# Gate projections by Strassen's seven products as well, sums of weights in one chain per set

## The chip, the core and the metric

The kernel runs on one core of a Trainium2 chip. The core has TensorE (PE: matrix products, its weight loads shown as PEld), VectorE (DVE), ScalarE (ACT), GpSimd (POOL) and SyncE (SP, which here only starts DMA transfers). They run side by side and wait for each other by semaphores; each takes its own instructions in order. The metric is the device time of one execution in microseconds (us), the median of several runs.

## The reference

A two-layer encoder on 512 tokens of width 1024, all in float32. Each layer:

```
x = x + 0.5 * swiglu(rms_norm(x, ffn1_norm), w_gate, w_up, w_down)     # d_ff = 2816
z = rms_norm(x, mix_norm) @ w_in;  four attention mixers;  x = x + y @ w_out
x = x + 0.5 * swiglu(rms_norm(x, ffn2_norm), w_gate, w_up, w_down)
x = x + sigmoid(rms_norm(x, ple_norm) @ w_gate) * (p @ w_proj)
swiglu(u) = (silu(u @ w_gate) * (u @ w_up)) @ w_down
```

and a last RMSNorm. The change touches the two matrices `w_gate` and `w_up` of the four FFNs (two a layer).

## The kernel before

Tokens lie along the free dimension (512 columns), features along the 128 partitions. A float32 product is made of three matmuls of rounded operands: weights and activations are each split into a high and a low part, and high x high, high x low and low x high are accumulated (`mm3`, `product`). A weight block is loaded raw by SP and then **cut** (`cut`, L223): ScalarE writes the rounded high part `wh` (L231), VectorE subtracts it to get the low part `wl` (L232). There are three buffers of `wh` and three of `wl`. `take` hands a cut block to TensorE and prepares the next ones, two ahead in the FFN.

An FFN has 22 blocks of 128 gate and up columns, done in two halves of 12 and 10 blocks (`CUT`), each half followed by its part of the down projection (8 output tiles, each over the blocks `hs[0:4]`, `hs[4:8]`, `hs[8:]`). Blocks 0 and 1 of the first half are computed directly; meanwhile `combos` makes sums of activations in tiles TC. From then on blocks go in pairs (10 pairs per FFN, 40 in all). In a pair:

- **up** of both blocks goes by Strassen's scheme in Winograd's form (`seven`): the weights of the two blocks are a 2 x 2 matrix of 512 x 128 pieces a11, a12, a21, a22, the tokens are halved into 256 columns, and 7 products of 256 columns (named X1, Z1, X2, Y, X3, Z2, X4; each is 12 matmuls, L407) take the place of 8. Three PSUM banks X, Y, Z collect them; X takes four products, read out between them. ScalarE and VectorE put the results together in `u` (L422 to L434).
- **gate** of both blocks is direct: 4 half blocks of 12 matmuls with 512 columns (L298 to L300), then `gate` per block: multiplication by the norm factor `rb` (L440), Tanh (L442), one scalar_tensor_tensor (L443).
- `ORDER` = "ssdssdssdsd" sets how TensorE goes through the 7 products (s) and the 4 direct halves (d). The first block is multiplied by up and split for the down projection after Z2 (L514), the second at the end (L516).

The products need sums of weight pieces. `sums` and `factors` make them by DMA: SP loads a piece into a buffer `y` (L249), and accumulating DMAs, which only the POOL queue issues, add others (L251, L266): S1 = a21 + a22, S2 = S1 + a11 in a buffer of its own, S3 = a11 + a21, S4 = S2 + a12 in S2's buffer. That is five accumulations per pair. The `y` tag has four buffers.

What sets the order: instructions of TensorE and SP stay as written (`manual_schedule`). Those of the other engines are ordered at build time by a list scheduler, which takes older instructions first among those that it counts as ready; `hold` keeps the written order only in the opening. SP therefore stops at a load whose buffer isn't free, and all later loads wait behind it.

Of the kernel before, what the change touches and what calls it, by code (L numbers as in the profile page):

```python
# [17 lines left out]
T = 512  # L18
KC = 8
FF = 22  # L20
HT = 256
CUT = (0, 12, 22)
S_STEPS = ("X1", "Z1", "X2", "Y", "X3", "Z2", "X4")
ORDER = "ssdssdssdsd"
EPS = 1e-6
BIG = 1e30
NT_MIX = 20
# [10 lines left out]
class Encoder:  # L38
# [47 lines left out]
        return self.tile("keep", [128, 2, T], F32R, 7)  # L86

    def ytile(self):
        return self.tile("y", [128, T], F32, 4)

    def dense(self):
        return self.ps.tile([128, T], F32, tag="ps", name=self.nm("ps"), bufs=3)

    def small(self):
        return self.ps.tile([128, T], F32, tag="s", name=self.nm("s"), bufs=4)

    def either(self):
        self.turn ^= 1
# [19 lines left out]
    def setup_mix(self):  # L118
        nc, a, c = self.nc, self.a, self.const
        self.sink = c.tile([128, self.depth, 4], F32, name="sink")  # L120
        nc.sync.dma_start(self.sink, a["sink"])
        self.nsink = c.tile([128, self.depth, 4], F32, name="nsink")
        nc.gpsimd.tensor_scalar(out=self.nsink, in0=self.sink, scalar1=-1.0, scalar2=None, op0=ALU.mult)
        self.na_mask = c.tile([128, 7, 16], F32, name="na_mask")
        nc.sync.dma_start(self.na_mask, a["na_mask"])
        self.swa_mask = c.tile([128, 384], F32, name="swa_mask")
        nc.sync.dma_start(self.swa_mask, a["swa_mask"])
        self.dil_mask = c.tile([128, 896], F32, name="dil_mask")
        nc.sync.dma_start(self.dil_mask, a["dil_mask"])
        self.klz = [c.tile([128, 2, T], F32R, name=f"klz{i}") for i in range(2)]  # L130
        self.nkl = 0
        for t in self.klz:
            nc.gpsimd.memset(t[64:128, 0].bitcast(F32), 0.0)
            nc.gpsimd.memset(t[0:64, 1].bitcast(F32), 0.0)

    def g(self, l, off, k):
        c = l * GAINS + off + k
# [17 lines left out]
    def plan(self):  # L155
        a = self.a
        full = ((0, 4, 128), (512, 4, 128))
        for l in range(self.depth):
            for w in range(2):
                gu = a["ffn_gu"][l, w]  # L160
                for half in range(2):
                    c0, c1 = CUT[half], CUT[half + 1]
                    for f in range(c0, c1, 2):
                        if f == 0:
                            for n, g in enumerate(self.direct(l == w == 0, gu)):
                                yield g
                                if n == 4:
                                    sums = self.sums(gu[2, 1], gu[3, 1])
                            continue
                        s = self.factors(gu[f, 1], gu[f + 1, 1], sums)  # L170
                        d = self.slices((gu[f, 0], full), (gu[f + 1, 0], full))
                        for n, c in enumerate(ORDER):
                            yield s if c == "s" else d
                            if n == 3 and f + 2 < FF:
                                sums = self.sums(gu[f + 2, 1], gu[f + 3, 1])
                    for m in range(KC):
                        dn = a["ffn_d"][l, w, m]
                        yield from self.each((dn[:, c0:c0 + 8], full), (dn[:, c0 + 8:c1], ((0, c1 - c0 - 8, 128),)))
                if w == 0:
                    for i in range(M_END):  # L180
# [32 lines left out]
    def opening_pieces(self, gu):  # L213
        nc, a = self.nc, self.a
        for i, (k, e, xs) in enumerate(((0, 0, (0,)), (0, 1, (1, 2, 3)), (4, 0, (4,)), (4, 1, (5, 6, 7)))):
            raw = self.raw()[:, 0:512]
            src = gu[0, e][:, k:k + 4]
            nc.sync.dma_start(raw, src.rearrange("p k m -> p (k m)"))
            for m in xs:
                nc.sync.dma_start(self.x[m], a["x"][:, m])  # L220
            yield self.cut(raw, 4, self.own("TC", [128, 2, T], F32R, 8))

    def cut(self, r, k, both=None):  # L223
        nc = self.nc
# [13 lines left out]
            for o, k, m in cuts:  # L238
                yield self.cut(raw[:, o:o + k * m], k)

    def sums(self, a, b):

        flat = lambda src, k: src[:, k:k + 4].rearrange("p k m -> p (k m)")
        a11, a12, a21, a22 = flat(a, 0), flat(a, 4), flat(b, 0), flat(b, 4)
        nc = self.nc

        def load(first, *more):
            t = self.ytile()
            nc.sync.dma_start(t, first)  # L249
            for src in more:  # L250
                nc.gpsimd.dma_start(t, src, accum_op=ALU.add)  # L251
            return t

        s1 = load(a21, a22)
        s2 = load(a21, a22, a11)
        return s1, s2, lambda: load(a11, a21), a12

    def factors(self, a, b, sums):
        s1, s2, third, a12 = sums
        raw, half = self.load(a), self.raw()  # L260
        yield self.cut(raw[:, 0:512], 4)
        s3 = third()
        yield self.cut(s1, 4)
        self.nc.sync.dma_start(half[:, 0:512], b[:, 4:8].rearrange("p k m -> p (k m)"))
        yield self.cut(s2, 4)
        self.nc.gpsimd.dma_start(s2, a12, accum_op=ALU.add)  # L266
        yield self.cut(raw[:, 512:1024], 4)
        yield self.cut(s3, 4)
        yield self.cut(s2, 4)
        yield self.cut(half[:, 0:512], 4)  # L270

    def side(self):
        return self.nc.gpsimd if self.mixing else self.nc.vector
# [65 lines left out]
    def rspread(self, rc, tag="rb", bufs=1):  # L339
        nc = self.nc  # L340
        bc = self.spread(rc)
        rb = self.own(tag, [128, T], F32, bufs) if tag == "P" else self.tile(tag, [128, T], F32, bufs)
        nc.scalar.activation(rb, bc, AF.Copy)  # L343
        return rb

# [28 lines left out]
    def combos(self, l, off, j):  # L374
# [9 lines left out]
        nc.vector.scalar_tensor_tensor(f[:, 3], f[:, 2], -1.0, q[:, 2], op0=ALU.mult, op1=ALU.subtract)  # L384
        out = []
        for i in (0, 2):
            t = self.own("TC", [128, 2, T], F32R, 8).rearrange("p e (h t) -> p e h t", h=2)
# [22 lines left out]
    def seven(self, xs, tn, u):  # L410

        nc = self.nc
        bank = {}
# [49 lines left out]
    def ffn(self, l, w, nxt):  # L463
# [4 lines left out]
        tn, held = [], []  # L468
        for half in range(2):
            nf = CUT[half + 1] - CUT[half]  # L470
            hs = [self.big() if f < 7 else self.keep() for f in range(nf)]
            for f in range(2 if half == 0 else 0):
                gp, up = self.dense(), self.small()
                if l == w == f == 0:
# [16 lines left out]
            if half == 0:  # L491
                tn = [self.combos(l, off, j) for j in range(4)]
            for f in range(0 if half else 2, nf, 2):
                u = self.keep().bitcast(F32)
                s = self.seven(xs, tn, u)
                gps, grs, nd = [None] * 2, [None] * 2, 0
                for c in ORDER:
                    if c == "d":
                        e, part = divmod(nd, 2)
                        nd += 1  # L500
                        if part == 0:
                            gps[e] = self.dense()
                            self.mm3(gps[e], self.take(), xs[0:4], stop=False)
                            continue
                        self.mm3(gps[e], self.take(), xs[4:8], start=False)
                        grs[e] = self.gate(gps[e], rb)
                        continue
                    name = next(s)
# [4 lines left out]
                    if name == "Z2":  # L513
                        nc.vector.tensor_tensor(grs[0], grs[0], u[:, 0], op=ALU.mult)  # L514
                        self.split(hs[f], grs[0])
                nc.vector.tensor_tensor(grs[1], grs[1], u[:, 1], op=ALU.mult)  # L516
                self.split(hs[f + 1], grs[1])
            if self.sink is None:
                self.setup_mix()
            if half:  # L520
# [142 lines left out]
    def pv(self, h, b):  # L663
        nc, odd = self.nc, h["odd"]
        if b == 0:
            h["pv"] = self.ps.tile([128, T], F32, tag="pv", name=self.nm("pv"), bufs=1)
        pv = h["pv"]
        t0, t1 = self.span(h, b)
        c = slice(t0 * 128, t1 * 128)
# [224 lines left out]
    def mix(self, l, nxt):  # L894
# [244 lines left out]
def _prepare(i):  # L1139
# [7 lines left out]
    gu[:, :, 2:, 1] = gu[:, :, 2:, 1][:, :, :, :, [0, 2, 4, 6, 1, 3, 5, 7]]  # L1147
# [64 lines left out]
```

## Time and profile before

| | |
|---|---|
| median of 3 runs | 2111.67 us (2108.23 to 2111.96) |
| profiled execution | 2106.58 us |
| its span, first to last instruction | 2104.8 us |
| TensorE busy | 2058.1 us (98%), granted clock 0.995 |
| VectorE, ScalarE, POOL busy | 65%, 52%, 19% |
| DMA | 269.07 MB, 128 GB/s in the mean |

"Busy" counts the time in which an engine has at least one instruction running. Matmuls overlap in their pipeline, so the duration of one is longer than the time from its start to the next start. The four FFNs with their Strassen stretches lie at about 33 to 135 and 203 to 310, 660 to 768 and 830 to 938, 1075 to 1177 and 1243 to 1350, 1700 to 1805 and 1871 to 1977 us; behind each lies its part of the down projection.

### The profile page before, as it was taken

The page shows a single profiled execution, that of the slowest core. Times are in us where ns is not written, and L with a number is a line of the kernel's source. Part 1 is how long each engine was busy: PE and PEld are TensorE (multiplying, and loading weights), DVE is VectorE, ACT ScalarE, POOL GpSimd, SP SyncE. Part 2 cuts the span into 40 slices and gives each one's busy share as a digit, 9 for nine tenths or more (in the row PEclk, how much of TensorE's full clock was granted, in tenths as well). Part 3 has the DMA queues.
Part 4 walks back from the last instruction along what each step waited for, and adds up shares of the span by engine and source line. Part 5 has one row for each costly group of instructions (what it writes and reads, how often), then busy time and mean ns, then how long its engine had stood idle before and what let it go on. Part 6 is the DMA issues. An engine that isn't in the chain of part 4 may idle for free.

```text
span 2104.8 us, 29990 instructions
## 1 busy us (share of the span) xinstructions
PE 2058.1 (98%) x11012; PEld 1762.0 (84%) x11012; DVE 1364.0 (65%) x2269; ACT 1086.1 (52%) x2054; POOL 391.6 (19%) x390
## 2 busy tenths in 40 slices
PE   8999999999999999999999999999999899999997
PEld 7988988887877988988889889888878689889886
DVE  7654666778777654666866546667777766546664
ACT  6442444687864442444644334447787645334443
POOL 2200101043222200101121002011423312012011
PEclk9999999999999999999999999999999999999998
DMA  7764753322125754753467457433121367458332
GB/s 221 178 166 116 185 137 113 95 66 81 60 71 133 196 138 127 184 135 103 129 152 184 126 142 182 119 107 107 60 67 61 87 163 181 121 138 196 110 100 78
DMA packets 109605, 269.07 MB, mean 128 GB/s; under 512 B 12689, under 2 KB 16913, under 8 KB 109457
## 3 DMA queue, kind: packets, MB, share of 16 engines
q1 hardware_dynamic: 79232, 208.89, 31.4%
q0 software_dynamic: 30080, 58.21, 16.3%
q8 instruction: 86, 1.41, 0.3%
q14 instruction: 63, 0.51, 0.1%
q10 hardware_dynamic: 144, 0.05, 0.0%
HBM read 262.91 MB, written 2.10 MB: 126 GB/s over the span
## 4 chain that ended last, share of the span: by engine, by line
PE 43%; DVE 4%; ACT 1%; issue 1%; DMA 1%; POOL 0%; POOLq 0%; DVEq 0%; SPq 0%; ACTq 0%
PE s L407 8%; PE ps L299 7%; PE ps L298 7%; PE ps L300 7%; PE s L298 3%; PE s L299 3%; PE s L300 3%; PE ps L407 1%; PE pv L672 1%; PE s L656 1%; ACT tmp L542 0%; DVE PT L660 0%; PE s L614 0%; PE s L615 0%; DVE act L565 0%
## 5 line engine op out<-in xcount | busy, mean ns | idle before, releaser
L231 ACT ACTIVATE wh<-raw 128x512 fp32r<-128x512 f32 (+2 forms) x668 | 407.4, 612 | 569.1 <-PE ps L299 245.5
L232 DVE TENSOR_TENSOR wl<-raw,wh 128x512 fp32r<-128x512 f32 (+2 forms) x594 | 416.8, 703 | 258.3 <-ACT wh L231 251.1
L251 POOL DMA_DIRECT2D y<-in_ffn_gu x160 | 139.1, 878 | 909.0 <-DMA y<-in_ffn_gu 512.8
L298 PE MATMUL ps<-big,wh 128*128 128x512 f32 x632 | 252.4, 399 | 0.0
L299 PE MATMUL ps<-big,wh 128*128 128x512 f32 x632 | 247.9, 392 | 2.0 <-DVE big L152 2.0
L300 PE MATMUL ps<-big,wl 128*128 128x512 f32 x632 | 247.4, 391 | 1.6 <-DVE wl L232 1.6
L298 PE MATMUL ps<-act,wh 128*128 128x512 f32 x624 | 248.8, 399 | 0.0
L300 PE MATMUL ps<-act,wl 128*128 128x512 f32 x624 | 244.1, 391 | 1.4 <-DVE wl L232 1.4
L299 PE MATMUL ps<-act,wh 128*128 128x512 f32 x624 | 244.4, 392 | 0.6 <-DVE act L152 0.6
L407 PE MATMUL s<-TC,wh 128*128 128x256 f32 x1280 | 236.1, 282 | 0.7 <-ACT rb L343 0.7
L407 PEld LDWEIGHTS s<-TC,wh 128*128 128x128 f32 x1280 | 205.7, 189 | 10.3 <-ACT rb L343 0.9
L232 DVE TENSOR_TENSOR wl<-y,wh 128x512 fp32r<-128x512 f32 x160 | 110.8, 693 | 127.2 <-ACT wh L231 125.4
L407 PE MATMUL s<-TC,wl 128*128 128x256 f32 x640 | 181.4, 283 | 0.0
L231 ACT ACTIVATE wh<-y 128x512 fp32r<-128x512 f32 x160 | 101.2, 633 | 154.4 <-DMA y<-in_ffn_gu 60.7
L300 PEld LDWEIGHTS ps<-big,wl 128*128 128x128 f32 x632 | 118.6, 188 | 28.5 <-DVE wl L232 2.7
L300 PEld LDWEIGHTS ps<-act,wl 128*128 128x128 f32 x624 | 117.1, 188 | 27.3 <-DVE wl L232 1.8
L299 PEld LDWEIGHTS ps<-big,wh 128*128 128x128 f32 x632 | 119.2, 189 | 22.8 <-DVE big L152 3.1
L232 POOL TENSOR_TENSOR wl<-raw,wh 128x512 fp32r<-128x512 f32 (+1 forms) x74 | 95.8, 1295 | 216.2 <-ACT wh L231 210.0
L298 PEld LDWEIGHTS ps<-big,wh 128*128 128x128 f32 x632 | 119.2, 189 | 19.9
L299 PEld LDWEIGHTS ps<-act,wh 128*128 128x128 f32 x624 | 117.6, 188 | 20.8 <-DVE act L152 1.3
L298 PEld LDWEIGHTS ps<-act,wh 128*128 128x128 f32 x624 | 117.5, 188 | 19.6
L314 POOL TENSOR_TENSOR acc<-acc,tmp 128x512 f32<-128x512 f32 x48 | 66.9, 1394 | 344.7 <-ACT tmp L313 344.5
(230 smaller groups left out, 4343.9 us busy)
## 6 DMA issues: line engine op xcount, KB each, us to landing
raw<-in_ffn_gu SPq DMA_DIRECT2D x134, 512.0 KB, 5.1
y<-in_ffn_gu POOLq DMA_DIRECT2D x200, 256.0 KB, 4.9
raw<-in_ffn_d SPq DMA_DIRECT2D x64, 512.0 KB, 3.5
y<-in_ffn_gu SPq DMA_DIRECT2D x120, 256.0 KB, 3.9
raw<-in_w_in SPq DMA_DIRECT2D x40, 512.0 KB, 3.6
raw<-in_ffn_gu SPq DMA_DIRECT2D x44, 256.0 KB, 3.7
raw<-in_ffn_d SPq DMA_DIRECT2D x32, 256.0 KB, 2.7
raw<-in_w_out SPq DMA_DIRECT2D x16, 512.0 KB, 3.5
```

Of the source, the lines that this page charges most:

```text
L231: self.hold(nc.scalar.activation(hi, r, AF.Copy))
L232: self.hold(self.side().tensor_tensor(out=lo, in0=r, in1=hi.bitcast(F32), op=ALU.subtract))
L251: nc.gpsimd.dma_start(t, src, accum_op=ALU.add)
L298: nc.tensor.matmul(ps, lhsT=wh[:, k], rhs=x[:, 0], start=start and k == 0, stop=False)
L299: nc.tensor.matmul(ps, lhsT=wh[:, k], rhs=x[:, 1], start=False, stop=False)
L300: nc.tensor.matmul(ps, lhsT=wl[:, k], rhs=x[:, 0], start=False, stop=stop and k == last)
L314: self.hold(eng.tensor_tensor(out=acc, in0=acc, in1=sq, op=ALU.add))
L407: nc.tensor.matmul(ps, lhsT=v[:, k], rhs=x[:, e], start=start and k == i == 0, stop=k == 3 and i == 2, skip_group_check=True)
L656: nc.tensor.transpose(tp[:, t * 128:(t + 1) * 128], h["P"][t][:, o:o + 128], self.ident)
L672: nc.tensor.matmul(pv[:, c], lhsT=vb, rhs=h["pt"][b][:, i, c], start=b == 0 and i == 0, stop=b == 3 and i == 1, skip_group_check=True)
```

## The change

Gate goes through `seven` as well, as a second set with a buffer `g` beside `u`, and the products of the two sets take turns (up, gate, up, ...): 14 products per pair in place of 7 products and 4 direct halves. The order within a set becomes Z1, X1, Y, X2, X3, Z2, X4. The multiplication by `rb`, Tanh, the product with `u` and the split come after the fourteenth product, for both blocks together (1024 columns for the two multiplications). Gate's Y uses the bank `pv`, which only the mixer used.

The sums of a set share one buffer from a new tag S with seven buffers: S1 = a21 + a22, then a11 is added in place by DMA after S1 was cut, then a12 is added in place by VectorE after S2 was cut. S3 has its own buffer, and a22 is loaded alone. That is three accumulations per set, six per pair. The first two loads of the next pair's chains are issued after the eighth take of a pair. Buffers y, S, TC and klz now belong to stages (klz is cleared in each mixer stage), and the gate weights are laid out in DRAM as up's.

```diff
-S_STEPS = ("X1", "Z1", "X2", "Y", "X3", "Z2", "X4")
-ORDER = "ssdssdssdsd"
+S_STEPS = ("Z1", "X1", "Y", "X2", "X3", "Z2", "X4")
...
-                        s = self.factors(gu[f, 1], gu[f + 1, 1], sums)
-                        d = self.slices((gu[f, 0], full), (gu[f + 1, 0], full))
-                        for n, c in enumerate(ORDER):
-                            yield s if c == "s" else d
-                            if n == 3 and f + 2 < FF:
-                                sums = self.sums(gu[f + 2, 1], gu[f + 3, 1])
+                        fs = [self.factors(gu[f, i], gu[f + 1, i], chains[i]) for i in range(2)]
+                        for n in range(14):
+                            yield fs[1 - n % 2]
+                            if n == 7 and f + 2 < FF:
+                                chains = self.chains(gu, f + 2)
...
+    def block(self, *srcs):
+
+        t = self.own("S", [128, T], F32, 7)
+        for i, src in enumerate(srcs):
+            self.more(t, src, i > 0)
+        return t
+
+    def more(self, t, src, add=True):
+        src = src.rearrange("p k m -> p (k m)")
+        if add:
+            self.nc.gpsimd.dma_start(t, src, accum_op=ALU.add)
+        else:
+            self.nc.sync.dma_start(t, src)
+
+    def chains(self, gu, f):
+        c = [None, None]
+        for i in (1, 0):
+            b = gu[f + 1, i]
+            c[i] = self.block(b[:, 0:4], b[:, 4:8])
+        return c
+
+    def factors(self, a, b, s):
+        raw = self.load(a)
+        yield self.cut(s, 4)
+        self.more(s, a[:, 0:4])
         yield self.cut(raw[:, 0:512], 4)
+        s3 = self.block(a[:, 0:4], b[:, 0:4])
         yield self.cut(raw[:, 512:1024], 4)
+        a22 = self.block(b[:, 4:8])
+        yield self.cut(s, 4)
+        self.nc.vector.tensor_tensor(out=s, in0=s, in1=raw[:, 512:1024], op=ALU.add)
         yield self.cut(s3, 4)
+        yield self.cut(s, 4)
+        yield self.cut(a22, 4)
...
-                bank[b] = (self.dense() if b == "Y" else self.small())[:, :HT]
+                bank[b] = (self.small() if b == "X" else self.dense() if b == "Z" or first else self.extra())[:, :HT]
...
-            hs = [self.big() if f < 7 else self.keep() for f in range(nf)]
+            hs = [self.big() if f < 8 else self.keep() for f in range(nf)]
...
+                u, g = self.keep().bitcast(F32), (self.keep() if f % 4 else self.pair()).bitcast(F32)
+                su, sg = self.seven(xs, tn, u, True), self.seven(xs, tn, g, False)
+                for _ in S_STEPS:
+                    next(su)
                     if rc is not None:
                         rb, rc = self.rspread(rc), None
                         for j, hj in enumerate(held):
                             self.gated(*hj, rb, hs[j])
+                    next(sg)
+                nc.vector.tensor_tensor(g, g, rb.unsqueeze(1).to_broadcast([128, 2, T]), op=ALU.mult)
+                for e in range(2):
+                    th = self.tmp()
+                    nc.scalar.activation(th, g[:, e], AF.Tanh, scale=0.5)
+                    nc.vector.scalar_tensor_tensor(g[:, e], th, 1.0, g[:, e], op0=ALU.add, op1=ALU.mult)
+                nc.vector.tensor_tensor(g, g, u, op=ALU.mult)
+                for e in range(2):
+                    self.split(hs[f + e], g[:, e])
...
         self.stage("mx")
+        self.clear()
```

## Rows read from the trace of the kernel before

**Rows 1.** The page, part 1: busy us, share of the span, instructions.

```profile
PE 2058.1 (98%) x11012; PEld 1762.0 (84%) x11012; DVE 1364.0 (65%) x2269; ACT 1086.1 (52%) x2054; POOL 391.6 (19%) x390
```

**Rows 2.** Busy us by stretch (Strassen, down, Strassen); then PEclk, DMA share, GB/s.

```profile
60.00:121.00 61.00, 61.00 (x385) 55.28 (x384) 38.29 (x64) 29.04 (x54) 11.89 (x15) 1.00 0.76 187
145.00:195.00 50.00, 50.00 (x223) 41.40 (x221) 19.73 (x31) 12.02 (x19) 0.90 (x1) 1.00 0.37 108
1099.00:1161.00 62.00, 62.00 (x390) 56.10 (x389) 39.54 (x65) 30.67 (x56) 12.00 (x14) 1.00 0.76 184
```

**Rows 3.** Instructions in order of time, TensorE: start, duration in us, instruction, count.

```profile
82.37 0.40 PE L407 MATMUL s<-TC,wh 128*128 128x256 f32 x2
...
83.81 0.40 PE L407 MATMUL ps<-act,wh 128*128 128x256 f32 x2
...
85.24 0.40 PE L298 MATMUL ps<-act,wh 128*128 128x512 f32 x1
...
87.99 0.40 PE L407 MATMUL s<-TC,wh 128*128 128x256 f32 x2
```

**Rows 4.** The same view: VectorE at the pair's end, and one cut.

```profile
79.59 0.69 DVE L516 TENSOR_TENSOR tmp<-tmp,keep 128x512 f32<-128x512 f32 x1
...
83.93 0.63 ACT L231 ACTIVATE wh<-y 128x512 fp32r<-128x512 f32 x1 [0.90 <-PE s L407]
...
84.60 0.69 DVE L232 TENSOR_TENSOR wl<-y,wh 128x512 fp32r<-128x512 f32 x1 [0.84 <-ACT wh L231]
...
85.32 0.33 SPq L249 DMA_DIRECT2D y<-in_ffn_gu  x1
...
100.65 0.68 DVE L516 TENSOR_TENSOR tmp<-tmp,keep 128x512 f32<-128x512 f32 x1
```

**Rows 5.** Groups by line and shape: busy us, mean ns of one.

```profile
L232 DVE TENSOR_TENSOR wl<-y,wh 128x512 fp32r<-128x512 f32 x160 | 110.8, 693 | 127.2 <-ACT wh L231 125.4
...
L428 DVE TENSOR_TENSOR keep<-keep,ps 128x256 f32<-128x256 f32 x40 | 16.8, 421 | 6.2 <-PE ps L407 6.2
...
L865 DVE TENSOR_TENSOR raw<-na_mask,raw 128x896 f32<-128x896 f32 x8 | 8.7, 1090 | 1.6 <-DMA raw<-in_na_bias 1.6
...
L231 ACT ACTIVATE wh<-y 128x512 fp32r<-128x512 f32 x160 | 101.2, 633 | 154.4 <-DMA y<-in_ffn_gu 60.7 <-PE s L407 56.2 <-PE ps L300 13.4
...
L426 ACT ACTIVATE keep<-s 128x256 f32<-128x256 f32 x40 | 14.7, 367 | 0.0
```

**Rows 6.** In order of time, VectorE back to back.

```profile
109.36 0.69 DVE L232 TENSOR_TENSOR wl<-y,wh 128x512 fp32r<-128x512 f32 x1 [2.44 <-ACT wh L231]
109.96 0.69 DVE L440 TENSOR_TENSOR tmp<-ps,rb 128x512 f32<-128x512 f32 x1
...
111.16 0.42 DVE L430 TENSOR_TENSOR keep<-keep,s 128x256 f32<-128x256 f32 x1
111.49 0.69 DVE L443 SCALAR_TENSOR_TENSOR tmp<-tmp,tmp 128x512 f32<-128x512 f32 x1
```

**Rows 7.** The page, part 3: queue, packets, MB, share of 16 engines' span.

```profile
q1 hardware_dynamic: 79232, 208.89, 31.4%
q0 software_dynamic: 30080, 58.21, 16.3%
```

**Rows 8.** In order of time: SP's loads into y, POOL's accumulations waiting for them.

```profile
71.52 4.31 SPq L249 DMA_DIRECT2D y<-in_ffn_gu  x2
...
76.17 0.86 POOL L251 DMA_DIRECT2D y<-in_ffn_gu  x1 [5.90 <-DMA y<-in_ffn_gu]
...
91.66 5.23 SPq L249 DMA_DIRECT2D y<-in_ffn_gu  x2
...
95.80 0.86 POOL L251 DMA_DIRECT2D y<-in_ffn_gu  x1 [4.78 <-DMA y<-in_ffn_gu]
```

**Rows 9.** From issue to landing: L266 (x40) first, L251 (x160) second.

```profile
DMA to landing us min/median/max: 3.7/6.6/8.2
...
DMA to landing us min/median/max: 3.5/4.6/8.2
```

More of the change, by code (lines that the diff above doesn't have):

```diff
@@ L88, in ytile @@
     def ytile(self):
-        return self.tile("y", [128, T], F32, 4)
+        return self.own("y", [128, T], F32, 4)
     def dense(self):
@@ L95, in small, with extra, pair @@
         return self.ps.tile([128, T], F32, tag="s", name=self.nm("s"), bufs=4)
+    def extra(self):
+        return self.ps.tile([128, T], F32, tag="pv", name=self.nm("pv"), bufs=1)
+    def pair(self):
+        return self.own("TC", [128, 2, T], F32R, 9)
     def either(self):
@@ L129, in setup_mix, with clear @@
         nc.sync.dma_start(self.dil_mask, a["dil_mask"])
-        self.klz = [c.tile([128, 2, T], F32R, name=f"klz{i}") for i in range(2)]
+    def clear(self):
+        self.klz = [self.own("klz", [128, 2, T], F32R, 2) for _ in range(2)]
         self.nkl = 0
         for t in self.klz:
-            nc.gpsimd.memset(t[64:128, 0].bitcast(F32), 0.0)
-            nc.gpsimd.memset(t[0:64, 1].bitcast(F32), 0.0)
+            self.nc.gpsimd.memset(t[64:128, 0].bitcast(F32), 0.0)
+            self.nc.gpsimd.memset(t[0:64, 1].bitcast(F32), 0.0)
     def g(self, l, off, k):
@@ L166, in plan @@
                                 yield g
-                                if n == 4:
-                                    sums = self.sums(gu[2, 1], gu[3, 1])
+                                if n == (4 if l == w == 0 else 6):
+                                    chains = self.chains(gu, 2)
                             continue
-                        s = self.factors(gu[f, 1], gu[f + 1, 1], sums)
-                        d = self.slices((gu[f, 0], full), (gu[f + 1, 0], full))
-                        for n, c in enumerate(ORDER):
-                            yield s if c == "s" else d
-                            if n == 3 and f + 2 < FF:
-                                sums = self.sums(gu[f + 2, 1], gu[f + 3, 1])
+                        fs = [self.factors(gu[f, i], gu[f + 1, i], chains[i]) for i in range(2)]
[3 more added lines that the diff above has]
+                                chains = self.chains(gu, f + 2)
                     for m in range(KC):
@@ L220, in opening_pieces @@
                 nc.sync.dma_start(self.x[m], a["x"][:, m])
-            yield self.cut(raw, 4, self.own("TC", [128, 2, T], F32R, 8))
+            yield self.cut(raw, 4, self.pair())
     def cut(self, r, k, both=None):
@@ L239, in slices @@
                 yield self.cut(raw[:, o:o + k * m], k)
[L241 to L260, printed above, removed]
-        yield self.cut(raw[:, 0:512], 4)
[L262 to L266, printed above, removed]
+    def block(self, *srcs):
[19 more added lines that the diff above has]
+        self.more(s, a[:, 0:4])
+        yield self.cut(raw[:, 0:512], 4)
+        s3 = self.block(a[:, 0:4], b[:, 0:4])
         yield self.cut(raw[:, 512:1024], 4)
+        a22 = self.block(b[:, 4:8])
+        yield self.cut(s, 4)
+        self.nc.vector.tensor_tensor(out=s, in0=s, in1=raw[:, 512:1024], op=ALU.add)
         yield self.cut(s3, 4)
-        yield self.cut(s2, 4)
-        yield self.cut(half[:, 0:512], 4)
+        yield self.cut(s, 4)
+        yield self.cut(a22, 4)
     def side(self):
@@ L341, in rspread @@
         bc = self.spread(rc)
-        rb = self.own(tag, [128, T], F32, bufs) if tag == "P" else self.tile(tag, [128, T], F32, bufs)
+        rb = self.tile(tag, [128, T], F32, bufs) if tag == "rb" else self.own(tag, [128, T], F32, bufs)
         nc.scalar.activation(rb, bc, AF.Copy)
@@ L386, in combos @@
         for i in (0, 2):
-            t = self.own("TC", [128, 2, T], F32R, 8).rearrange("p e (h t) -> p e h t", h=2)
+            t = self.pair().rearrange("p e (h t) -> p e h t", h=2)
             nc.scalar.activation(t[:, :, 0], f[:, i:i + 2], AF.Copy)
@@ L408, in product, with seven @@
                                  stop=k == 3 and i == 2, skip_group_check=True)
-    def seven(self, xs, tn, u):
+    def seven(self, xs, tn, u, first):
         nc = self.nc
@@ L493, in ffn @@
             for f in range(0 if half else 2, nf, 2):
[L494 to L508, printed above, removed]
+                u, g = self.keep().bitcast(F32), (self.keep() if f % 4 else self.pair()).bitcast(F32)
+                su, sg = self.seven(xs, tn, u, True), self.seven(xs, tn, g, False)
+                for _ in S_STEPS:
+                    next(su)
                     if rc is not None:
@@ L512, in ffn @@
                             self.gated(*hj, rb, hs[j])
[L513 to L517, printed above, removed]
+                    next(sg)
[7 more added lines that the diff above has]
+                    self.split(hs[f + e], g[:, e])
             if self.sink is None:
@@ L665, in pv @@
         if b == 0:
-            h["pv"] = self.ps.tile([128, T], F32, tag="pv", name=self.nm("pv"), bufs=1)
+            h["pv"] = self.extra()
         pv = h["pv"]
@@ L1146, in _prepare @@
     gu = gu.reshape(L, 2, 2, KC, 128, FF, 128).transpose(0, 1, 5, 2, 4, 3, 6).copy()
-    gu[:, :, 2:, 1] = gu[:, :, 2:, 1][:, :, :, :, [0, 2, 4, 6, 1, 3, 5, 7]]
+    gu[:, :, 2:] = gu[:, :, 2:][:, :, :, :, :, [0, 2, 4, 6, 1, 3, 5, 7]]
     r["ffn_gu"] = gu
```

## The prediction

> **What bounds the kernel now.** I read the page's engine line first, then the busy time by stretch, then the order of time inside one pair of gate and up blocks, and last the DMA views. TensorE is busy 98% of the span [rows 1]. In the Strassen stretches it is busy in every one of the 61 or 62 us at a granted clock of 1.00, VectorE in 38 to 40 of them, ScalarE in 29 to 31, with the DMA engines at 76% [rows 2]. So in these stretches a weight or a buffer that comes late is not what ends a wait: the number of columns that TensorE streams sets the time. That is what the change cuts, and the question is which of the others then comes too late.
>
> One product of Strassen (12 matmuls of 256 columns) takes 1.435 us (82.37 to 83.81 to 85.24), one half of a direct gate block (12 of 512 columns) 2.75 us (85.24 to 87.99) [rows 3]. A pair is 7 products and 4 halves: 10.05 + 11.00 = 21.05 us; the same line comes back after 21.06 us (79.59 to 100.65) [rows 4]. L428 runs once in a pair, and its row counts 40 [rows 5]: 842 us of the 2104.8.
>
> **TensorE, part by part.** Each pair loses 4 halves (11.00 us) and gains 7 products (10.05 us): 20.10 us in place of 21.05, 0.95 us less, 38 us over 40 pairs. The number of products doubles; their price is the row's own and not half of a 512-column one.
> The Trainium skill ("TensorE: Matmul & The Clock Gate", Back-to-back issue gap) gives a matmul some 2.5 ns beside its columns, so a 256-column one would be 109 ns and a 512-column one 216. The trace has 120 and 229 (1.435/12, 2.75/12) and doesn't agree. By the page the gain would be 48 x 216 - 84 x 109 ns = 1.2 us a pair, 48 us in all.
>
> **VectorE and ScalarE.** A pair has 11 cuts (ScalarE rounds a weight block, VectorE subtracts) and will have 14. A VectorE instruction of 512 columns takes 0.69 us, of 256 columns 0.42 [rows 5]; back to back they start 0.60 and 0.33 us apart [rows 6]. Two rows, 512 columns in 0.69 and 896 in 1.09, put a 1024-column one at about 1.22 us (an estimate). After the change a pair has 14 subtractions, 2 additions S+a12, 6 combinations of 256 columns, two 1024-column multiplications, 2 scalar_tensor_tensor and 2 subtractions of the split: 20 x 0.60 + 6 x 0.33 + 2 x 1.13 = 16.2 us back to back, 18.8 at full durations. Both lie under 20.1, so VectorE isn't the bound on average. ScalarE: 18 x 0.63 + 8 x 0.37 = 14.3 us, hidden.
>
> What matters is the order inside a pair. A cut can begin 0.12 us after a product starts (its buffer is one of three) and is over 1.48 us after it (83.81; 83.93; 84.60 + 0.69) [rows 3, 4]. The product that needs it starts 2.87 us after, so 1.39 us are spare. Now the nonlinear chain of both blocks stands at the end of the pair, where it was spread over it: multiplication by rb (1.22), Tanh, two scalar_tensor_tensor, multiplication by u (1.22), split. If the second scalar_tensor_tensor and the multiplication by u go ahead of a waiting subtraction, it loses 0.60 + 1.13 = 1.73 us, 0.34 more than is spare. Bounds: 0 and 0.34 us a pair. I take 0.15, since each cut that gets between them removes it: 6 us over 40 pairs.
>
> The reads of PSUM: in `seven` the second and the third product of bank X now have one product of the other set between them (1.435 us), where 4.2 us of work stood. Between them ScalarE must copy 256 columns (0.37 us [rows 5]), and it is asked before the next cut, so about 0.9 us remain. I count 0; a cut of 0.63 ahead of it would still fit.
>
> **Ends of the halves.** After the last product of a half comes the whole chain: copy 0.37, multiplication 1.22, Tanh 0.63, two scalar_tensor_tensor 0.69 + 0.60, multiplication 1.22, first copy of the split 0.63, hand-offs of about 0.05 each: hs[f] is there after 5.7 us, its low half after 6.4, hs[f+1] 0.6 later. The down matmuls run 0.224 us each (223 in 50 us) [rows 2]. In the half of 10 blocks hs[8] is wanted after 24 of them, 5.4 us, and its low half one later: 0.3 to 0.8 us late, and 0.6 more for each cut that goes between. I take 1.2 for each of the 4 halves, 5 us; bounds 0.3 and 2. In the half of 12, hs[10] is wanted after 6.7 us and hs[11] after 7.4: hidden, late by under 0.5. Before, hs[f] was done earlier and only one multiplication, Tanh, one more and the split followed.
> At the first pair of the first FFN, the gate's Z bank is one of the three "ps" banks, of which two still hold the opening's gates: it must wait for one VectorE read after rb, about 0.7 us. Clearing klz in each mixer stage is four small memsets on POOL, which is busy 19% of the span [rows 1], well ahead of the first read: 0.
>
> **The weights' sums.** Bytes of a pair: SP's queue carries 2.5 MiB as before (four loads of 256 KiB and three of 512, then six and two), the POOL queue 6 accumulations of 256 KiB in place of 5. From the queue shares a MB costs 3.16 us of all 16 engines on q1 (31.4% of 2104.8 us for 208.89 MB) and 5.89 on q0 [rows 7]: 2.62 x 3.16 + 1.57 x 5.89 = 17.6 us of 20.1, 87%; the same sum for before gives 16.0 of 21.05, 76%, as the stretch shows. So bandwidth is not the bound, but transfers will stand in each other's way longer.
>
> The wait to watch is the new buffer pool S. A pair takes 6 of 7 buffers, so the gate's sum for the next pair (the second of `chains`) must wait for the buffer of up's S3, cut at take 8 of 14 (from 0). SP is behind it in its own order, with both 512 KiB loads of the next pair, and POOL's accumulation waits for it. It is wanted by take 15. From the start of product 6 to that of product 15 are 9 x 1.435 = 12.9 us. The SP issue comes 1.51 us after the first (83.81 to 85.32) and the cut takes 1.36 [rows 3, 4], so load and accumulation may take 10.0 us. Load to start of the accumulation is 4.1 to 4.7 us (91.66 to 95.80, 71.52 to 76.17) [rows 8]; the accumulation lands after 3.5 to 8.2 us, median 4.6 at L251, 6.6 at L266 [rows 9]. 4.4 + 4.6 + 0.1 = 9.1: in time by 0.9. I take this end, since these are accumulations onto a fresh load as at L251; SP's queue will have drained while it waited, too. With 6.6 it is 11.1, 1.1 late, and that end is kept. The other accumulation with a due time, S1 += a11, has from take 0 to take 6: 6 x 1.435 = 8.6 us, where 6.6 and two hand-offs fit. S += a12, a DMA before (L266, the slow one), is now one VectorE instruction; TensorE never waited for it, so nothing is gained by it.
>
> **Sum.** -38 + 6 + 5 + 0.7 = -26 us. The profiled execution took 2106.58 us (span 2104.8), so 2080.3; it lies 5.1 under the median of three, 2111.67, and from that median the forecast is **2085.5 us**.
>
> **Rivals.**
> *The S chain binds (slower).* Place: the gate's first cut of a pair. With 4.65 us for the load and 6.6 for the accumulation it takes 11.35 us against 10.0, 1.35 us a pair. The first pair of each half has its sums loaded long before, so 32 pairs count: 43 us, 2128. It decides from 26/32 = 0.8 us, a chain of 10.8 us. For it: 87% of the DMA engines' time taken, and L266's 6.6. Against it: the median of L251's 160 accumulations is 4.6.
> The Trainium skill ("DMA: Bandwidth & Descriptors", Issuing engines are not separate DMA queues) says that transfers started by any engine run on the same 16 DMA engines and interleave, so a load on SP's queue can hold an accumulation of POOL's up. L266's landings, up to 8.2 us, fit that [rows 9].
> *VectorE's order binds.* Both chain pieces go ahead of two subtractions, 0.7 us a pair, 28 in place of 6: 2107. For it: 81 to 94% of VectorE's time would be taken. Against it: TensorE lost nothing at 63%, and ScalarE's Tanh leaves gaps in the chain for cuts.
> *The full step.* Scheduling hides chain and ends: -38, 2073.
> *Half the columns at half the price.* If 256-column matmuls, with no 512-column ones between, came to half of 0.229 us, 168 of them would be 19.25 us, 1.8 us less a pair: 72 in place of 38, 2051. Against it: the second product of [rows 3] stands behind another and takes 1.43 us all the same. I give it 0.02.
> The Trainium skill's section on the issue gap, named above, has the two prices at about one to two.
>
> **How the numbers follow.** Forecast with its own range 2073 to 2097 (the full step included): 0.62. VectorE's order, 2097 to 2112: 0.14, of which 0.10 is faster and 0.04 same. The S chain: 0.22, of which 0.18 slower and 0.04 a draw, since it may bind by less. The half price: 0.02. Faster 0.62 + 0.10 + 0.02 = 0.74, same 0.08, slower 0.18; 0.2% is 4.2 us, about what a measurement of this kernel can tell from no change. The range goes from the full step, 2072, to 2116, which leaves out the S chain where it binds fully and the half price.
>
> **What would show it.** Right: L407 products of 1.43 us back to back, TensorE still busy in all of a Strassen stretch, a pair every 20.1 to 20.5 us, VectorE near 80%, a gap of 1 us before hs[8] in the half of 10. Wrong: ScalarE waiting on a DMA for S with a TensorE gap once a pair behind it (S chain); gaps in TensorE ended by L232 with VectorE full in the first third of a pair (VectorE's order); a pair of 21 us or more.

## The result, and the profile after

The changed kernel is slower: 2164.47 us median (2161.58 to 2168.13) against 2111.25 of the kernel before, ratio 1.026 (95% interval 1.0248 to 1.0273). The forecast was 2085.5, the range 2072 to 2116. The profiled execution has a span of 2162.9 us, 58.1 more than before. In its code the products stand at L417, the cut at L237 (ScalarE) and L238 (VectorE), SP's loads into S at L259, POOL's accumulations at L257, S + a12 at L277 and the nonlinear part at L513 to L518.

The page after, engine line, queues and the chain (these answer to [rows 1] and [rows 7]):

```profile
PE 2062.3 (95%) x12452; PEld 1813.2 (84%) x12452; DVE 1517.5 (70%) x2509; ACT 1186.3 (55%) x2334; POOL 432.3 (20%) x434
...
q1 hardware_dynamic: 84992, 208.90, 29.2%
q0 software_dynamic: 35840, 68.70, 18.2%
...
PE 66%; DMA 15%; DVE 11%; ACT 5%; issue 3%; POOL 0%; SPq 0%; POOLq 0%; DVEq 0%; ACTq 0%
DMA S<-in_ffn_gu 13%; PE s L417 12%; PE ps L309 7%; PE ps L308 7%; PE ps L310 7%; PE ps L417 6%; PE s L310 6%; PE s L309 6%; PE s L308 6%; DVE wl L238 3%; PE pv L417 3%; PE pv L675 2%; ACT wh L237 2%; PE s L659 1%; ACT tmp L545 1%
```

The chain of waits runs through loads and accumulations of S for 13% of the span. The busy time of [rows 2] is now, for the same three stretches:

```profile
60.00:121.00 61.00, 57.97 (x466) 55.94 (x466) 49.32 (x81) 35.41 (x73) 12.77 (x15) 1.00 0.74 181
145.00:195.00 50.00, 49.51 (x223) 40.62 (x222) 23.94 (x35) 14.59 (x25) 0.00 (x0) 1.00 0.36 109
1099.00:1161.00 62.00, 59.11 (x453) 56.23 (x452) 45.88 (x75) 35.24 (x71) 12.34 (x14) 1.00 0.61 145
```

TensorE, which filled all of a Strassen stretch, stands still for 3 us in 60. VectorE is busy 81% of the first one (49.32 of 61), about as forecast. The DMA share didn't rise (0.74 against 0.76, 0.61 against 0.76): the transfers come late, they don't fill the engines.

What it comes to, from the starts of TensorE's matmuls: the first pair of a half, whose sums were loaded long before, takes 20.06 us (forecast 20.10; the very first, in the opening, 24.14), the 32 later ones 22.76 in the mean. I count products of a pair from 0 and call "lost at product n" what passes between its start and the next product's beyond 1.43 us. A later pair loses 1.14 us at product 0 (TensorE waits for gate's S1, which is product 1), 0.67 at 1, 0.28 at 5, 0.47 at 7 and 0.18 at the others: 2.74. A product starts as soon as ScalarE's high part is there; its third matmul needs VectorE's low part, so a late subtraction stops TensorE inside the product, as at 1, 5 and 7. Forty pairs at 20.02 in place of 21.05 gain 41 us; 32 x 2.74 = 88 are lost, the ends of the halves and the opening make up the rest of the 58.

One pair shows it. VectorE, ScalarE, SP and POOL from product 6 (88.71) to the next pair's product 1 (103.56):

```profile
88.21 0.68 DVE L156 TENSOR_TENSOR big<-TC,big 128x512 fp32r<-128x512 f32 x1
...
88.71 0.40 PE L417 MATMUL s<-TC,wh 128*128 128x256 f32 x2
88.79 0.64 ACT L237 ACTIVATE wh<-S 128x512 fp32r<-128x512 f32 x1 [0.32 <-PE pv L417]
88.81 0.68 DVE L277 TENSOR_TENSOR S<-S,raw 128x512 f32<-128x512 f32 x1
...
89.42 0.68 DVE L156 TENSOR_TENSOR big<-TC,big 128x512 fp32r<-128x512 f32 x1
...
90.02 0.68 DVE L238 TENSOR_TENSOR wl<-S,wh 128x512 fp32r<-128x512 f32 x1
...
90.62 0.41 DVE L438 TENSOR_TENSOR keep<-keep,pv 128x256 f32<-128x256 f32 x1
90.75 0.38 PE L417 MATMUL s<-TC,wl 128*128 128x256 f32 x1 [0.22 <-DVE wl L238]
...
90.95 1.28 DVE L238 TENSOR_TENSOR wl<-S,wh 128x512 fp32r<-128x512 f32 x2
91.66 0.33 SPq L259 DMA_DIRECT2D S<-in_ffn_gu  x1
92.04 0.90 SPq L216 DMA_DIRECT2D raw<-in_ffn_gu  x2
93.06 5.06 SPq L259 DMA_DIRECT2D S<-in_ffn_gu  x5
...
95.54 0.86 POOL L257 DMA_DIRECT2D S<-in_ffn_gu  x1 [12.20 <-DVE keep L440]
...
102.88 0.63 ACT L237 ACTIVATE wh<-S 128x512 fp32r<-128x512 f32 x1 [3.10 <-DMA S<-in_ffn_gu]
...
103.56 0.50 PE L417 MATMUL ps<-TC,wh 128*128 128x256 f32 x2 [1.37 <-ACT wh L237]
104.29 0.38 PE L417 MATMUL ps<-TC,wl 128*128 128x256 f32 x1 [0.23 <-DVE wl L238]
```

ScalarE has cut up's S3 at 89.43 (88.79 + 0.64), but VectorE gets to its subtraction at 90.95, after the split of the finished pair (L156 twice), S + a12, the cut before it and a combination. That subtraction frees the buffer for which SP waits: gate's load goes at 91.66, its accumulation at 95.54, ScalarE can cut the sum at 102.88, and TensorE has stood still for 1.4 us when it starts. Beside the accumulation run two loads of 512 KiB and five of 256 that SP had been holding back and issued within 6.5 us of its release (92.04 to 98.1). The wait at 90.75 is the other loss: product 7 has gate's S2, whose low part VectorE subtracts at 90.02, behind the same work.

### The profile page after: what moved, and what is told of

The parts are those of the page before. It is cut to its first block, busy times and chain, and to the rows that moved or that the text cites. A ratio compares the mean times of both kernels' runs of the same rounds, so it can differ in the third digit from the quotient of the medians.

```text
span 2162.9 us, 33791 instructions
## 1 busy us (share of the span) xinstructions
PE 2062.3 (95%) x12452; PEld 1813.2 (84%) x12452; DVE 1517.5 (70%) x2509; ACT 1186.3 (55%) x2334; POOL 432.3 (20%) x434
## 4 chain that ended last, share of the span: by engine, by line
PE 66%; DMA 15%; DVE 11%; ACT 5%; issue 3%; POOL 0%; SPq 0%; POOLq 0%; DVEq 0%; ACTq 0%
DMA S<-in_ffn_gu 13%; PE s L417 12%; PE ps L309 7%; PE ps L308 7%; PE ps L310 7%; PE ps L417 6%; PE s L310 6%; PE s L309 6%; PE s L308 6%; DVE wl L238 3%; PE pv L417 3%; PE pv L675 2%; ACT wh L237 2%; PE s L659 1%; ACT tmp L545 1%
## 5 line engine op out<-in xcount | busy, mean ns | idle before, releaser
L237 ACT ACTIVATE wh<-raw 128x512 fp32r<-128x512 f32 (+1 forms) x548 | 331.3, 606 | 386.1 <-PE ps L309 165.1
L238 DVE TENSOR_TENSOR wl<-raw,wh 128x512 fp32r<-128x512 f32 (+2 forms) x474 | 333.4, 704 | 196.8 <-ACT wh L237 194.3
L237 ACT ACTIVATE wh<-S 128x512 fp32r<-128x512 f32 x400 | 252.0, 632 | 323.4 <-PE s L417 123.1
L257 POOL DMA_DIRECT2D S<-in_ffn_gu x240 | 211.4, 1021 | 985.3 <-DVE wl L238 417.4
L238 DVE TENSOR_TENSOR wl<-S,wh 128x512 fp32r<-128x512 f32 x400 | 273.1, 690 | 178.6 <-ACT wh L237 167.2
L417 PE MATMUL s<-TC,wh 128*128 128x256 f32 x1920 | 347.1, 282 | 0.0
L417 PEld LDWEIGHTS s<-TC,wh 128*128 128x128 f32 x1920 | 295.1, 189 | 0.4
L417 PE MATMUL s<-TC,wl 128*128 128x256 f32 x960 | 273.5, 285 | 7.4 <-DVE wl L238 7.4
L417 PEld LDWEIGHTS s<-TC,wl 128*128 128x128 f32 x960 | 180.6, 188 | 13.2 <-DVE wl L238 13.1
L417 PE MATMUL ps<-TC,wh 128*128 128x256 f32 x640 | 124.6, 291 | 33.4 <-ACT wh L237 31.9
L238 POOL TENSOR_TENSOR wl<-raw,wh 128x512 fp32r<-128x512 f32 (+1 forms) x74 | 96.3, 1302 | 214.5 <-ACT wh L237 207.8
L417 PEld LDWEIGHTS ps<-TC,wh 128*128 128x128 f32 x640 | 101.0, 193 | 40.2 <-ACT wh L237 38.0
L308 PE MATMUL ps<-big,wh 128*128 128x512 f32 x328 | 133.1, 406 | 0.0
L309 PE MATMUL ps<-big,wh 128*128 128x512 f32 x328 | 128.3, 391 | 3.0 <-DVE big L159 3.0
L308 PE MATMUL ps<-act,wh 128*128 128x512 f32 x320 | 130.5, 408 | 0.0
L310 PE MATMUL ps<-big,wl 128*128 128x512 f32 x328 | 128.6, 392 | 0.9 <-DVE wl L238 0.9
L309 PE MATMUL ps<-act,wh 128*128 128x512 f32 x320 | 125.4, 392 | 0.0
L417 PE MATMUL ps<-TC,wl 128*128 128x256 f32 x320 | 95.5, 299 | 7.1 <-DVE wl L238 7.1
L308 PE MATMUL ps<-keep,wh 128*128 128x512 f32 x232 | 94.5, 407 | 3.5 <-ACT keep L155 3.4
L309 PE MATMUL ps<-keep,wh 128*128 128x512 f32 x232 | 91.4, 394 | 2.0 <-DVE keep L156 2.0
```

The costliest lines, as they stand in the source:

```text
L237: self.hold(nc.scalar.activation(hi, r, AF.Copy))
L238: self.hold(self.side().tensor_tensor(out=lo, in0=r, in1=hi.bitcast(F32), op=ALU.subtract))
L257: self.nc.gpsimd.dma_start(t, src, accum_op=ALU.add)
L308: nc.tensor.matmul(ps, lhsT=wh[:, k], rhs=x[:, 0], start=start and k == 0, stop=False)
L309: nc.tensor.matmul(ps, lhsT=wh[:, k], rhs=x[:, 1], start=False, stop=False)
L310: nc.tensor.matmul(ps, lhsT=wl[:, k], rhs=x[:, 0], start=False, stop=stop and k == last)
```

## The experiments

Ratios are to the kernel before, run beside each (2109 to 2111 us).

**Eight buffers.** S gets one more, for which one attention mask moves from the constants to the mixer stage.

```diff
...
-        t = self.own("S", [128, T], F32, 7)
+        t = self.own("S", [128, T], F32, 8)
```

> Theory S (the gate's sum for the next pair waits for a seventh buffer's release, and its load and accumulation then come too late): with eight buffers that load no longer waits for up's S3. The gaps at the first two products of a pair (1.9 us in the mean in 32 pairs, 60 us in all) go, the others stay: 2164 - 60, some 2100 to 2115. Theory V (VectorE's chain at the end of the pair before holds the first cuts up): nothing changes, 2155 to 2170. (The mask of the sliding window moves into the mixer's stage to make room; one 192 KiB load more, 0 to 1 us.)

Measured: 2180.97 us, 1.0338 (1.0309 to 1.0368), slower than with seven and outside the ranges of both theories. Nothing is lost at products 0 and 1 any more (below 0.01 us), but 1.16, 1.28 and 0.74 at 5, 6 and 7. The order that the build gave POOL had changed too; its rows in this kernel:

```profile
75.15 0.86 POOL L257 DMA_DIRECT2D S<-in_ffn_gu  x1 [0.22 <-issue]
82.50 3.54 POOL L257 DMA_DIRECT2D S<-in_ffn_gu  x4 [6.49 <-DMA S<-in_ffn_gu]
97.20 0.86 POOL L257 DMA_DIRECT2D S<-in_ffn_gu  x1 [11.17 <-DMA S<-in_ffn_gu]
```

Each S1 += a11 now stands behind an accumulation of the next pair, whose load isn't there: four leave one after the other from 82.50 and land 4.7, 5.9, 6.6 and 7.4 us after their issue. So the buffer was the cause of one loss, and this run has another in its place.

**Raw loads ahead of the sums' loads**, seven buffers: the two 512 KiB loads of the next pair are issued in `chains` before S, to stand outside the burst.

```diff
+        r = [self.load(gu[f, i]) for i in (1, 0)]
         for i in (1, 0):
             b = gu[f + 1, i]
-            c[i] = self.block(b[:, 0:4], b[:, 4:8])
+            c[i] = r[1 - i], self.block(b[:, 0:4], b[:, 4:8])
...
```

> Seven buffers as in the changed kernel, but the two 512 KiB loads of the next pair stand on SP's queue ahead of the sums' loads, so that they neither wait with the gate's sum nor run beside its accumulation. Theory S with contention as its larger part: the accumulation lands in 4.6 to 5.5 us in place of 7.0 to 7.3, the gap of 1.9 us shrinks to under 0.4 in 32 pairs: 2105 to 2120. Theory S without contention (the start alone is too late): 2150 to 2165. Theory V: 2155 to 2170.

Measured: 2166.2 us, 1.0269 (1.0226 to 1.0313): no gain. Less is lost at 0 and 1 (0.50, 0.39), more at 5 to 7 (0.55, 0.28, 0.91). SP issues in order, so these loads now waited for their own buffers and held gate's S1 up (3.39 us after product 6 in place of 2.68, means of 32). Its accumulation did get shorter, 5.98 us in place of 7.26 (means of 32), so the loads beside it are part of its price; the later start and the losses at 5 to 7 took the gain back.

**No nonlinear part**: L513 to L518 and the split are replaced by four ScalarE copies.

```diff
-                nc.vector.tensor_tensor(g, g, rb.unsqueeze(1).to_broadcast([128, 2, T]), op=ALU.mult)
...
-                    self.split(hs[f + e], g[:, e])
+                    nc.scalar.activation(hs[f + e][:, 0], g[:, e], AF.Copy)
+                    nc.scalar.activation(hs[f + e][:, 1], u[:, e], AF.Copy)
```

> Leaves out the nonlinear part of 40 pairs: no multiplication by rb, no Tanh, no product with up; ScalarE copies gate and up into hs instead (as many ScalarE instructions, six VectorE instructions less per pair). Theory V: all gaps within the pairs go (2.7 us in 32 pairs) and the ends of the halves too: 2070 to 2085. Theory S: the gaps at the first two products stay at 1.5 us or more; what goes is the gap at the sixth product (0.3 us), perhaps the eighth (0.5), and 5 us at the ends: 2130 to 2155.

Measured: 2117.26 us, 1.0039 (1.0024 to 1.0054), 47 us less than the changed kernel and between the two theories' ranges. The losses at 5 and 7 are gone (0.03 and 0.00), those at 0 and 1 are 0.67 and 0.59. SP's load goes 1.99 us after product 6 in place of 2.68; the accumulation still takes 6.99. So VectorE's chain has two prices: subtractions that TensorE waits for, and a buffer freed late.

**Ten buffers**, both masks moved.

```diff
...
-        t = self.own("S", [128, T], F32, 7)
+        t = self.own("S", [128, T], F32, 10)
```

> Ten buffers in S (both masks of the mixers moved into their stage). Theory S: as with eight, or a few us better since S3 and a22 are loaded earlier too and the burst of loads spreads: 2085 to 2115. Theory V: 2155 to 2170. If eight help and ten do not help more, the one wait of the eighth buffer was all; if ten help much more, it was the burst.

Measured: 2124.08 us, 1.0067 (1.0049 to 1.0085), 9 us over the range of theory S. Only product 7 loses in the later pairs (1.00 us), and the opening pair 10 us. Here POOL's order put both S1 += a11 behind both accumulations of the next pair's S1.

**Written order**, seven buffers: the accumulations are kept in the order in which the code issues them, as TensorE's and SP's instructions are.

```diff
-            self.nc.gpsimd.dma_start(t, src, accum_op=ALU.add)
+            self.tc.keep_in_program_order(self.nc.gpsimd.dma_start(t, src, accum_op=ALU.add))
```

> Seven buffers, but POOL's accumulations keep the order in which they are written: both S1 += a11 of a pair ahead of its two S3 sums, the next pair's S1 last. Theory Q (POOL's queue: accumulations stand behind others that wait for a load or a cut): the gap at the eighth product (0.5 us, 16 us in 32 pairs) goes, the gaps at the first two (1.9 us) stay since the seventh buffer still comes late: 2140 to 2155. Theory V (VectorE's chain holds the cuts up by itself): no change, 2160 to 2170.

Measured: 2161.41 us, 1.0241 (1.0226 to 1.0256), and 2.78 us lost in a later pair: POOL's order is not what slows the changed kernel.

**Written order and ten buffers**, the last two edits together.

> Ten buffers and POOL's accumulations in written order. With ten buffers alone the only gap left within later pairs is 1.2 us at the eighth product, where S1 += a11 stood last on POOL's queue behind the next pair's sums. Theory Q: it goes, 2124 - 30 to 38 = 2086 to 2096 (the opening's 10 us stay). Theory V: it stays, 2118 to 2128.

Measured: 2079.71 us, 0.9854 (0.9839 to 0.9869), 6 us under the range of theory Q. Later pairs take 20.20 us, all of the loss at product 7.

**The same with the nonlinear part block by block**, in instructions of 512 columns.

```diff
-                nc.vector.tensor_tensor(g, g, rb.unsqueeze(1).to_broadcast([128, 2, T]), op=ALU.mult)
                 for e in range(2):
+                    nc.vector.tensor_tensor(g[:, e], g[:, e], rb, op=ALU.mult)
...
-                nc.vector.tensor_tensor(g, g, u, op=ALU.mult)
-                for e in range(2):
+                    nc.vector.tensor_tensor(g[:, e], g[:, e], u[:, e], op=ALU.mult)
                     self.split(hs[f + e], g[:, e])
```

> As e6, and the nonlinear part goes block by block with 512-column instructions, so that no VectorE instruction of 1.2 us stands ahead of a cut and hs[f] is split before hs[f+1]'s part begins. Theory Q: the pairs run at 20.1 already in e6, so only the halves' ends gain, 2 to 5 us: 2082 to 2093. Theory V: a gain of 0.3 us or more a pair beside that, 12 us or more under e6.

Measured: **2063.41 us, 0.9778 (0.9762 to 0.9795)**, the fastest of all. Its windows, for the first two of [rows 2]:

```profile
60.00:121.00 61.00, 61.00 (x514) 61.00 (x513) 53.79 (x93) 39.88 (x79) 16.06 (x22) 1.00 0.82 196
145.00:195.00 50.00, 50.00 (x222) 41.40 (x221) 20.15 (x31) 12.02 (x19) 0.00 (x0) 1.00 0.41 129
```

Pairs take 20.03 us with VectorE busy 88% (53.79 of 61). No wait is left at the end of a half of 12: its down stretch lasts 65.3 us as before the change, 66.4 in the changed kernel. Of the four halves of 10, two still lose 0.9 us. The 16 us against the run above are more than either theory's account: the pairs give 5, and what lies outside them 12.

**No accumulations**, seven buffers: POOL's accumulating DMAs are left out (the sums lack their second pieces); everything else is done.

```diff
-            self.nc.gpsimd.dma_start(t, src, accum_op=ALU.add)
+            pass
```

> Seven buffers, all 240 accumulating transfers left out (the sums S1, S2, S3 lack their DMA terms); loads, VectorE's addition, cuts and the nonlinear chain as in the changed kernel. Theory Q (accumulations come too late): the gaps at the first two products and at the eighth go, 2164 - 32 x 2.4 = 2080 to 2095. Theory V: most of the 2.7 us a pair stays, 2140 or more. If it lands between, both share.

Measured: 2078.42 us, 0.9847 (0.9832 to 0.9861). Later pairs 20.20 us, as with ten buffers in written order. Without accumulations, VectorE's chain costs 0.17 us a pair and seven buffers are enough.

**Eight buffers in written order**, the edit of the first experiment and that of the fifth.

> Eight S buffers (one mask moved into the mixer stage) and the accumulations kept in written order. Theory 'buffer and order together': one buffer more lets the gate's S1 load start when it is issued, and the written order keeps S1 += a11 ahead of the next pair's sums; pairs of about 20.2 us, 2080 us (2074 to 2090), no gaps at products 0 and 1, under 0.4 us at product 7. Rival 'it took the ten buffers': an accumulation still waits behind a load that waits for a buffer, pairs of 21.5 us or more, 2120 us or more.

Measured: 2084.87 us, 0.9885 (0.9871 to 0.99). Later pairs 20.40 us. SP and POOL in it, and its busy time in the first window:

```profile
86.79 6.61 SPq L259 DMA_DIRECT2D S<-in_ffn_gu  x6
93.45 0.89 SPq L216 DMA_DIRECT2D raw<-in_ffn_gu  x2
...
94.77 0.86 POOL L257 DMA_DIRECT2D S<-in_ffn_gu  x1 [14.47 <-DVE wl L238]
96.20 3.53 POOL L257 DMA_DIRECT2D S<-in_ffn_gu  x4 [0.56 <-DVE wl L238]
...
60.00:121.00 61.00, 60.98 (x508) 60.54 (x508) 52.36 (x85) 38.62 (x77) 16.05 (x20) 1.00 0.87 209
```

Accumulations are slower here than in the changed kernel, and it doesn't matter. From issue to landing, the changed kernel first:

```profile
DMA to landing us min/median/max: 3.6/5.8/8.9
```

```profile
DMA to landing us min/median/max: 3.6/7.7/10.9
```

Gate's S1 is now the last of six accumulations issued within 3.6 us: it takes 9.93 us (mean of 32), and still lands 9.49 us before its product starts. Up's S1 += a11, the first of the six, takes 6.68 and lands 3.07 before product 6. What decides is how early it goes: gate's load is issued 27 us before its product, 11.6 in the changed kernel (means of 32). The 0.4 us a pair that are left are lost at product 7 (0.32).

**Seven buffers, nonlinear part block by block**, the edit above alone.

> The changed kernel with seven buffers, only the nonlinear part done block by block in instructions of 512 columns. Theory 'VectorE's chain lengthens the sums': at most what leaving the chain out gave (47 us) and about half of it, some 2140 us (2125 to 2152), gaps at products 5 and 7 smaller, those at 0 and 1 still over 0.5 us a pair. Rival 'the chain costs only at the ends of halves': 2153 to 2160, gaps as in the changed kernel.

Measured: 2141.54 us, 1.015 (1.0134 to 1.0166), some 23 less than the changed kernel. The losses at 5 and 7 go (0.04, 0.03), 0.99 and 0.62 at 0 and 1 stay.

**Eight buffers, written order, block by block**, three of the edits above together.

> Eight buffers, written order, nonlinear part block by block. If eight do as well as ten: 2064 us (2059 to 2070), pairs of 20.05 us. If ten are needed, 2090 us or more.

Measured: 2067.33 us, 0.9799 (0.9783 to 0.9815), later pairs 20.08 us: eight buffers do nearly as well as ten.

**Gate's S1 without its accumulation**, seven buffers; its sum starts from a21 alone.

```diff
-            c[i] = self.block(b[:, 0:4], b[:, 4:8])
+            c[i] = self.block(b[:, 0:4], b[:, 4:8]) if i else self.block(b[:, 0:4])
```

> The changed kernel with seven buffers; only gate's S1 is loaded without its accumulation (a22 is not added there: 40 of 240 accumulations left out). Theory 'the disputed term': gate's S1 load comes late for want of a buffer, and the 7 us that its accumulation takes decide; without it the load alone is in time, the gaps at products 0 and 1 (1.1 and 0.7 us a pair) go, and the gap at product 7 falls below 0.1 us since gate's S1 is cut earlier: 2080 to 2110 us. Rival 'the load is late by itself' (no buffer, SP's burst): a gap at product 0 or 1 of 0.5 us or more stays, 2130 us or more. Second rival 'S1 += a11 is a cause of its own': gaps at 5 and 7 stay at 0.3 and 0.4 us, 2100 to 2110.

Measured: 2114.11 us, 1.0014 (1.0004 to 1.0024), 50 us less than the changed kernel with 40 of its 240 accumulations left out. Nothing is lost at 0 and 1, so it is the accumulation and not the late load alone that decides there. It came out above the 2080 to 2110 of the theory, because 0.81 us is lost at 7 (0.22 at 5, 0.19 at 6): the second rival holds beside it, though with other sizes. No run separates what the 0.81 is made of.

The times of the buffer and the order, side by side:

| S buffers | order given at build | written order | written, block by block |
|---|---|---|---|
| 7 | 2164.5 | 2161.4 | |
| 8 | 2181.0 | 2084.9 | 2067.3 |
| 10 | 2124.1 | 2079.7 | 2063.4 |

With seven, the order is worth nothing; with eight it is worth 96 us; in written order, the eighth buffer is worth 77.

## Why the prediction was wrong

**The step that failed** is that of the weights' sums: "load and accumulation may take 10.0 us ... 4.4 + 4.6 + 0.1 = 9.1: in time by 0.9". From product 6 to the next pair's product 1, without waits 12.9 us, the changed kernel shows (means of 32 pairs):

| | forecast | measured | pair shown above |
|---|---|---|---|
| product 6 to SP's issue | 1.51 | 2.68 | 2.95 |
| load until POOL starts | 4.4 | 3.61 | 3.88 |
| accumulation and hand-off | 4.7 | 7.34 | 7.34 |
| cut until TensorE starts | 1.36 | 0.69 | 0.68 |
| sum | 11.97 | 14.33 | 14.85 |

(The 0.69 is the high part alone; the low part follows inside the product, the 0.67 lost at product 1, and both together are the 1.36 of the forecast.) The accumulation is the term that was mis-sized most, by 2.6 us; with 4.7 in its place the sum is 11.7, in time. The issue, 1.2 late, is the next. I took the median of L251 [rows 9], because these too are accumulations onto a fresh load. The trace of before had the slow end too, 6.6 at L266, and I didn't ask which loads ran beside each. In the changed kernel the wait for the buffer dams SP up, and the accumulation that hangs on that wait meets all the loads that it let go. I had written that SP's queue "will have drained while it waited"; it is the other way round.
The Trainium skill ("DMA: Bandwidth & Descriptors", Issuing engines are not separate DMA queues) has transfers of all engines interleave on the same DMA engines. The trace agrees: of the changed kernel's accumulations that were issued with no other one under way, 12 had at most 1 MiB of SP's loads beside them (under way, or issued within 3 us) and landed after 3.9 us in the mean, 38 had more and took 7.1. An accumulation also waits for others: with ten buffers in written order, where gate's S1 is issued as the last of six, it takes 9.4 us (mean of 32) and is in time all the same.

**The second part of the failure** is that two rivals were weighed apart and came together. "The S chain binds" had the right place and about its price: 43 us forecast, 50 measured by leaving that accumulation out. "VectorE's order binds" had 0.7 us a pair; the changed kernel loses 0.28 + 0.47 at products 5 and 7. But they feed each other. The subtraction that stands behind the nonlinear part frees the buffer 1.2 us late (2.68 against 1.51), of which 0.7 go when that part is left out (1.99). The way back is argued and not shown by itself: the late sums push the cuts into the nonlinear part, and these then stand behind it; what the runs show is that the losses at 5 and 7 go without accumulations too (0.00 and 0.17). So the losses don't add up: leaving out the chain gives 47 us, gate's accumulation 50, all accumulations 86, and one more buffer with the written order 80. The step "VectorE's order" (0.15 us a pair) was right for sums in time: 0.17 without accumulations, 0.18 with ten buffers.

**S1 += a11** ("from take 0 to take 6: 6 x 1.435 = 8.6 us, where 6.6 and two hand-offs fit"): in the changed kernel its place in POOL's queue costs nothing that the written order gives back (3 us). The step left out that the queue is ordered at build time; with more buffers that decided (96 and 44 us).

**TensorE** (-38 us): right. First pairs take 20.06 us, and 20.03 are reached all through in the fastest kernel; a product of 256 columns keeps its 1.43 us, so "half the price" is out. The 109 and 216 ns that the prediction set beside the trace are given in the Trainium skill ("TensorE: Matmul & The Clock Gate", Back-to-back issue gap) for an isolated matmul, and not for a stream with a weight load before each matmul as here; the 48 us worked out from them say nothing of this kernel.

**Ends of the halves** (1.2 us for each half of 10, the half of 12 hidden): too low. Over the first 40 matmuls of the down projection, the changed kernel loses 1.9 and 1.6 us in turn against the kernel before in the halves of 10 (bounds 0.3 and 2), and 1.1 in each half of 12 (66.4 against 65.3 for its whole down stretch): 11.5 us in all, where 5 was forecast. Without the nonlinear part all of it goes. All that lies outside the Strassen stretches grew by 9.5 us, so the rest took 2 less.

**The opening** (0.7 us): the very first pair takes 24.1 us, 4.1 more than the first pairs of the other halves; in the kernel before it took 22.9, 1.9 more than the other pairs. The change costs 2.2 there.

With eight buffers and the written order the kernel takes 2084.9 us: the forecast was about right for a kernel in which the sums come in time, and these two conditions were what it had taken for granted. That it comes within 1 us is luck in part: there a later pair takes 20.40 us where 20.25 was forecast, and the terms outside the pairs have their own misses.

## What to carry to other kernels

When a pool has one buffer less than what is in flight, budget the refill from the last reader that frees the buffer, with what stands ahead of that reader on its engine, and take for the transfer the slow end of the rows: a released queue sends what it held back close together. Before a buffer is added, fix the order on the in-order queue that it feeds; otherwise the room may be used to put later work ahead of urgent work, as here with eight and ten buffers. Two rivals that feed each other get a case of their own, with both prices.

## What was not expected of the hardware

- Accumulating DMAs that POOL issues 0.53 us apart land 1.3 to 1.8 us apart (issued 82.50 to 84.11, landed at 87.16, 88.92, 90.21 and 91.54, with eight buffers): behind each other they take 4.7 to 7.4 us for the same 256 KiB.
- The changed kernel's DMA share was lower than before (0.61 against 0.76 in 1099 to 1161) and its transfers came later: a mean share says nothing of one transfer's due time. With eight buffers in written order it was 0.87 in 60 to 121 and TensorE was busy in 60.98 of the 61 us.
